# Seven products for eight in one projection of a decoder layer's finish, with two engines' order written by hand

## The chip, the cores and the metric

The kernel runs on one core of a Trainium2 chip. The metric is device microseconds of one execution, lower is better. Engines are named as the profile names them: PE is TensorE (PEld its weight loads), DVE is VectorE, ACT is ScalarE, POOL is GpSimd, SP is SyncE, which here issues nearly all DMAs. A line such as L258 is a line of the kernel before.

## What is computed

One decoder layer over 2048 tokens and 16 meta tokens, width 1024, in fp32. After an RMS norm and one wide input projection come two attention branches: stick-breaking attention (8 heads, width 512) and banded (sliding-window) attention with sinks (16 query heads, width 1024). The finish, cut to what matters here:

```python
y_sb = (o_sb * silu(sb_z)) @ w_branch_sb        # 512 -> 1024
y_sw = (o_sw * silu(sw_z)) @ w_branch_swa       # 1024 -> 1024, the banded branch
merged = sigmoid(g_sb) * y_sb + sigmoid(g_sw) * y_sw
h = h + merged @ w_out
return rms_norm(h, final_norm_gain)
```

## The kernel before

**Numbers.** Every fp32 operand of a matmul is split into a high and a low part of the type that TensorE takes at full rate: ScalarE copies (rounds) to `h`, VectorE subtracts to get `l`. A product of two operands is three matmuls: high by high, high by low, low by high. A matmul is 128 x 128 weights by 128 x 512 columns.

**Stages.** The tokens are four groups of 512 (`GT`), handled as two halves, `halves = ([2, 3], [0, 1])`. For both halves come the projections, the banded attention and the stick-breaking attention; their outputs (`ow` banded, `od` stick-breaking, two summands), the silu gates (`zw`, `zs`) and sigmoid gates (`gw`, `gs`) wait in HBM. Some gates of the first half are already computed by seven products for eight (`gate_pairs`, L1115). At the end of the second half's attention five gate weights are left (`gts[rest:]`, L1457), each for two groups: ten tiles of 24 matmuls (`gemm`, L457). In `use` (L613) ScalarE takes the sigmoid out of PSUM, VectorE multiplies for the last four weights (silu), and SP stores the tile. Beside them `gated` (L206) prepares the finish of half 0: it loads `ow` and `zw` into `tmp` buffers, which the gates use as well, multiplies them on VectorE and splits the result into two tiles of `ringl`, 32 tiles in all. `weights` (L178) splits a weight on ScalarE or GpSimd and also stores both parts in HBM (`kept`), so that half 1 loads them.

**The finish** (`finish`, L235) runs for half 0, then half 1. First the banded branch: for each of eight output tiles `d` of 128 features and each of the two groups, 8 k x 3 matmuls into one bank (`project`, L254; banks go round over three tags of two), then one VectorE multiplication with the gate `gw` gives `part[d, g]` (L286). `osb` holds the other branch's operands, made by `gated` at d = 3. Then `w_sb` for each d and group: project over 4 k, gate, add `part`, split into `merged` (L289 to L300), while `out_weights` (L265) loads and splits `w_out`. Then the output projection with residual and norm, in row tiles (L303 to L375). Half 1's operands are made by `gated_in_place` (L223) during half 0's output.

**What sets the order.** TensorE's order is the program's order throughout (`manual_schedule`). The order on the other engines, and on SP's queue, is laid down ahead of time by the planner, except in places where `manual_schedule` names an engine. Every queue is then worked in its order: an instruction that waits holds up those behind it. Buffers come from pools with a tag and a count (`bufs`): `ringl` 32 tiles, `ringr` 40, `small("a")` 6, `small("gt")` 3, `wh` and `wl` 3 each, `raw` 2, `tmp` 9, `xs` 4. The pool of `finish` lies where the normalised inputs `xh`, `xl` and `tmp` lay before.

## Time and profile before

| | |
|---|---|
| time, median of 3 runs | 2090.95 us (2090.8 to 2092.35) |
| profiled execution, its own time | 2093.26 us |
| its span | 2091.4 us |
| PE busy | 2076.3 us, 99% |
| DVE, ACT, POOL busy | 70%, 52%, 17% |
| granted TensorE clock | 0.999 |
| last five gates | 1593 to 1647 us |
| banded branch of half 0 | 1647.6 to 1734.6 us |

The span is the time from the first to the last instruction of the profiled execution. PE's busy time counts overlapping matmuls once. A busy share is an average over stages that have different limits, so what a stage can give is read in windows of time. "Idle before, releaser" in the rows names what ended an engine's wait.

### The profile page before, as it was taken

To read this page: it belongs to the slowest core of one execution; us is meant where nothing else is said; L and a number is where in the kernel's file an instruction comes from. 1 tells how busy PE (TensorE), PEld (TensorE's weight loads), DVE (VectorE), ACT (ScalarE), POOL (GpSimd) and SP (SyncE) were. 2 spreads that over 40 slices of the span, in tenths; PEclk is the share of its full clock that TensorE was granted. 3 is DMA by queue.
4 is the path that set the end of the run, shared out by engine and by line. 5 is a ranking of instruction groups with operands and counts; after the bars stand their busy time and mean duration, and the time that the engine had idled before them with its cause. 6 is when DMAs were issued, how large, how long until landed. Compare 5 with 4: busy or idle time off the path is not lost. (4 is left out here: it accounts for less than half of the span.)

```text
span 2091.4 us, 30949 instructions
## 1 busy us (share of the span) xinstructions
PE 2076.3 (99%) x10579; PEld 1744.8 (83%) x10579; DVE 1463.0 (70%) x2383; ACT 1091.4 (52%) x2657; POOL 345.7 (17%) x682
## 2 busy tenths in 40 slices
PE   9999999999999999999999999999999999999998
PEld 7888888888888888888888888888888888788887
DVE  7897986877687754887728788777774547464543
ACT  6677774577665335777735555655653212321121
POOL 1233444331000000233310000000000343000000
PEclk9999999999999999999999999999999999999999
DMA  9855555866377574435455344343424987568532
GB/s 338 307 195 201 188 175 179 252 199 185 91 278 298 209 247 163 159 126 177 150 171 161 120 130 129 114 129 98 121 83 165 350 318 223 182 229 305 154 100 91
DMA packets 170093, 391.46 MB, mean 187 GB/s; under 512 B 23728, under 2 KB 28208, under 8 KB 169936
## 3 DMA queue, kind: packets, MB, share of 16 engines
q1 hardware_dynamic: 169648, 389.23, 55.8%
q8 instruction: 83, 1.36, 0.3%
q14 instruction: 74, 0.61, 0.1%
q10 hardware_dynamic: 288, 0.27, 0.0%
HBM read 241.68 MB, written 145.18 MB: 185 GB/s over the span
## 5 line engine op out<-in xcount | busy, mean ns | idle before, releaser
L464 PE MATMUL ps_g<-xh,wh 128*128 128x512 f32 x1264 | 517.0, 409 | 1.1 <-DVE tmp L680 0.6
L464 PE MATMUL ps_g<-xl,wh 128*128 128x512 f32 x1264 | 495.6, 392 | 0.7 <-DVE xl L1199 0.6
L464 PE MATMUL ps_g<-xh,wl 128*128 128x512 f32 x1264 | 495.7, 392 | 0.0
L928 DVE TENSOR_TENSOR_SCAN row<-row 128x512 f32<-128x512 f32 (+4 forms) x256 | 290.1, 1134 | 116.2 <-POOL row L923 60.1
L464 PEld LDWEIGHTS ps_g<-xh,wl 128*128 128x128 f32 x1264 | 237.8, 188 | 52.7
L464 PEld LDWEIGHTS ps_g<-xh,wh 128*128 128x128 f32 x1264 | 238.5, 189 | 39.9 <-ACT xh L1198 1.4
L464 PEld LDWEIGHTS ps_g<-xl,wh 128*128 128x128 f32 x1264 | 239.2, 189 | 38.0 <-DVE xl L1199 1.8
L921 ACT ACTIVATE row<-ps_z 128x512 f32<-128x512 f32 (+4 forms) x352 | 175.1, 509 | 159.3 <-PE ps_z L918 155.0
L126 ACT ACTIVATE wth<-ps_t 128x512 fp32r<-128x512 f32 (+1 forms) x320 | 171.6, 536 | 61.4 <-PE ps_t L943 59.6
L127 DVE SCALAR_TENSOR_TENSOR wtl<-ps_t,wth 128x512 fp32r<-128x512 f32 (+1 forms) x320 | 188.7, 590 | 21.3 <-ACT wth L126 20.7
L918 PE MATMUL ps_z<-kt,q 128*128 128x512 f32 (+4 forms) x704 | 183.7, 349 | 2.0 <-ACT row L921 1.9
L943 PE MATMUL ps_t<-ident,row 128*128 128x128 f32 x1088 | 171.4, 273 | 1.0 <-DVE wtl L127 0.9
L943 PEld LDWEIGHTS ps_t<-ident,row 128*128 128x128 f32 x1088 | 134.5, 140 | 33.1 <-DVE wtl L127 1.8
L918 PEld LDWEIGHTS ps_z<-kt,q 128*128 128x128 f32 x704 | 124.4, 188 | 27.4 <-ACT row L921 5.1
L975 PE MATMUL ps_o<-wth,vc 128*128 128x512 f32 (+1 forms) x320 | 131.2, 410 | 0.0
L975 PE MATMUL ps_o<-wtl,vc 128*128 128x512 f32 (+1 forms) x320 | 116.4, 364 | 0.0
L767 ACT ACTIVATE sc<-sc,nm 128x129 f32<-128x129 f32 x256 | 100.0, 393 | 30.5 <-DVE nm L765 29.5
L934 POOL COPY mr<-row 128x16 f32<-128x16 f32 x128 | 28.4, 224 | 444.2 <-DVE row L928 401.8
L615 ACT ACTIVATE tmp<-ps_g 128x512 f32<-128x512 f32 x80 | 48.0, 600 | 80.5 <-PE ps_g L464 74.3
L299 ACT CAST ringl<-gt 128x512 fp32r<-128x512 f32 x32 | 19.9, 621 | 127.1 <-DVE gt L297 93.3
L117 POOL TENSOR_SCALAR wh<-raw 128x1024 fp32r<-128x1024 f32 (+1 forms) x45 | 49.8, 1108 | 212.7 <-PE ps_g L464 90.3
L123 POOL TENSOR_TENSOR wl<-raw,wh 128x256 fp32r<-128x256 f32 x88 | 83.2, 975 | 2.0
(442 smaller groups left out, 4202.3 us busy)
## 6 DMA issues: line engine op xcount, KB each, us to landing
wh<-h_in_w_in SPq DMA_DIRECT2D x66, 512.0 KB, 3.9
wl<-l_in_w_in SPq DMA_DIRECT2D x66, 512.0 KB, 5.1
h_in_w_in<-wh SPq DMA_DIRECT2D x50, 512.0 KB, 3.3
l_in_w_in<-wl SPq DMA_DIRECT2D x50, 512.0 KB, 4.1
raw<-in_w_in SPq DMA_DIRECT2D x49, 512.0 KB, 5.3
q<-qd SPq DMA_DIRECT2D x128, 128.0 KB, 3.2
vc<-vd SPq DMA_DIRECT2D x48, 256.0 KB, 3.2
kd<-tmp SPq DMA_DIRECT2D x32, 256.0 KB, 3.4
```

The lines of the kernel that those rows point to most:

```text
L117: G.tensor_scalar(h, src, 1.0, 1.0, op0=ALU.mult, op1=ALU.mult)
L123: G.tensor_tensor(l[:, c], src[:, c], f32(h[:, c]), op=ALU.subtract)
L126: A.activation(h, acc, AF.Copy, scale=scale)
L127: V.scalar_tensor_tensor(l, acc, scale, f32(h), op0=ALU.mult, op1=ALU.subtract)
L464: T.matmul(acc, lhsT=a[:, k, :], rhs=b[:, k, :], start=k == i == 0, stop=k == KT - 1 and i == 2)
L615: A.activation(e, acc, AF.Sigmoid)
L767: A.activation(sc[:, hh, :], sc[:, hh, :], AF.Exp, bias=nm[:, hh:hh + 1], accum_out=den[:, hh:hh + 1])
L918: T.matmul(z[:, :m], lhsT=qt[:, j * P:(j + 1) * P], rhs=kt[h][:, k0 + c:k0 + c + m], start=t == 0, stop=t == 1)
L921: A.activation(r[:, c:c + m], z[:, :m], AF.Sigmoid, scale=-1.0)
L928: V.tensor_tensor_scan(r[:, :w], r[:, :w], r[:, :w], last[j] if n else 1.0, op0=ALU.mult, op1=ALU.min)
L943: T.transpose(tr[:, j * P:(j + 1) * P], rows_of[h, g, n - (j > i), j][:, k0:k0 + P], ident)
L975: T.matmul(o[:, :n], lhsT=v, rhs=r, start=first and r is wh, stop=last)
```

## The change

For half 0 the banded branch is no longer computed as 16 independent tiles. Two output tiles d and d + 1 by the two groups ga and gb form a 2 x 2 square, and the 1024 features of k are cut in two halves of four (`HK`). Each square is a 2 x 2 by 2 x 2 block product, done with seven block products of 12 matmuls and sums of operands (Winograd's form): four squares, 28 products. `branch_by_pairs` holds TensorE's order, with sums left in a PSUM bank (`za`, `zb`, `x`) and continued by a later product.

- `outputs_blocks` makes the operands: for each of four k it loads four `ow`/`zw` pairs straight into ring tiles, multiplies, forms the sums t1 to t4 and splits them. Seven of these (t4 of every k, t3 of k = 2 and 3, t2 of k = 3) are written to HBM instead (`away`) and loaded and split later in `finish` (`late_split`).
- `weight_blocks` and `fill` make the weights' sums and split them on ScalarE and VectorE; GpSimd has no part in it. `w_sw` is no longer kept in HBM: half 1 loads it raw and splits it again (`keep=False`).
- A step of `outputs_blocks` (or a fill) follows each of the ten last gate tiles in program order. From the first of these to the branch's end ScalarE's and VectorE's order is the program's order.
- The other branch's operands (`other_branch`) are loaded and made between the products; the order of the gates' loads is written out (`gates`).
- `ringl` has 43 tiles, `ringr` 29; tiles of the branch's results and of `w_out` are shared out between them. `fg`'s load is moved behind the branch. In the `w_sb` loop tiles 0 and 1 go together, as (0, ga), (1, ga), (0, gb), (1, gb), and the last product of the branch stands behind the first of these. In half 1 loads of `w_sw` and `gw` are issued behind the last load of `w_out`.

```diff
-    def weights(c0, w=w_in, raw=None, split=split):
+    def weights(c0, w=w_in, raw=None, split=split, keep=True):
...
+        if not keep:
+            return wh, wl
...
+    def outputs_blocks(blk, away, k, ga, gb, ring, stg, free):
+        names = "b11", "b21", "t1", "b22"
+        here = [*names, "t2", "t3"][:(6, 6, 5, 4)[k]]
+        for name in here:
+            blk[name, k] = ring(), ring()
+        for name, kk, g in (("b11", k, ga), ("b21", k + HK, ga), ("t1", k, gb), ("b22", k + HK, gb)):
+            for t, src in zip(blk[name, k], (ow, zw)):
+                DMA(f32(t), src[kk][g])
+        yield
+        b11, b21, b12, b22 = (stg() for _ in names)
+        for t, name in zip((b11, b21, b12, b22), names):
+            a, z = blk[name, k]
+            V.tensor_tensor(t, f32(a), f32(z), op=ALU.mult)
+            if name in ("b11", "b21"):
+                part_split(*blk[name, k], t)
+        yield
+        t3 = free()
+        V.tensor_tensor(t3, b22, b12, op=ALU.subtract)
+        V.tensor_tensor(b12, b12, b11, op=ALU.subtract)
+        part_split(*blk["t1", k], b12)
+        part_split(*blk["b22", k], b22)
+        V.tensor_tensor(b22, b22, b12, op=ALU.subtract)
+        V.tensor_tensor(b21, b21, b22, op=ALU.subtract)
+        for name, t in (("t2", b22), ("t3", t3), ("t4", b21)):
+            if name in here:
+                part_split(*blk[name, k], t)
+            else:
+                away[name, k] = dram(f"{name}{k}", [P, GT])
+                DMA(away[name, k], t)
...
+        def gated_sum(d, g, acc):
+            t = part[d, g]
+            gt = gate_of(d, g)
+            V.tensor_tensor(t, acc, t, op=ALU.add)
+            V.tensor_tensor(t, t, gt, op=ALU.mult)
+        def close(d, z, w):
+            gt = gate_of(d, ga)
+            product(z, w, "t4", stop=True)
...
+            product(za, w[1], "t2")
+            keep(a, gb, za)
+            w = step()
+            product(x, w[0], "b22", stop=True)
+            gated_sum(a, gb, x)
+            middle()
+            product(za, w[1], "t3")
+            gated_sum(a + 1, gb, za)
+            w = step()
+            x = bank()
+            product(x, w[0], "t1", True)
+            keep(b + 1, gb, x)
+            middle()
+            close(a + 1, za, w[1])
...
+                def other_branch(k, g, ring):
+                    a, b, c = (small("a", AB) for _ in range(3))
+                    for t, src in ((a, od[k][g][0]), (c, od[k][g][1]), (b, zs[k][g])):
+                        DMA(t, src)
+                    V.tensor_tensor(a, a, c, op=ALU.add)
+                    V.tensor_tensor(a, a, b, op=ALU.mult)
...
-            osw = {}
-            todo = [(k, g) for g in halves[0] for k in range(8)]
...
+            byhand.enter_context(tc.manual_schedule(engines={mybir.EngineType.Activation, mybir.EngineType.DVE}))
+            next(side)
+            made_w = [gts[rest]()]
+            for mk in (*gts[rest + 1:], None):
+                if mk:
+                    made_w.append(mk())
+                w, use, _ = made_w.pop(0)
+                for g in groups:
+                    drain(lagged(col_tile(w, g, use)))
+                    next(side)
```

In the code `step` calls `before`, which makes the next fill of weights (fourteen fills, each for two products), and `middle` calls `during`, which holds the late splits and the other branch.

## The prediction

> **What bounds the kernel now.** I read the page's busy times first, then the windows around the stage that changes.

> ```profile
> span 2091.4 us, 30949 instructions
> ...
> PE 2076.3 (99%) x10579; PEld 1744.8 (83%) x10579; DVE 1463.0 (70%) x2383; ACT 1091.4 (52%) x2657; POOL 345.7 (17%) x682
> ```

> ```profile
> core 0: us, PE busy (x) PEld busy (x) DVE busy (x) ACT busy (x) POOL busy (x), PEclk, DMA share, GB/s
> 1590.00:1620.00 30.00, 30.00 (x136) 24.82 (x135) 7.85 (x12) 7.22 (x15) 0.00 (x0) 1.00 0.67 221
> 1620.00:1647.00 27.00, 27.00 (x121) 22.36 (x120) 18.59 (x24) 8.13 (x15) 9.97 (x10) 1.00 0.94 338
> 1647.00:1690.00 43.00, 43.00 (x192) 35.59 (x191) 20.64 (x25) 6.08 (x9) 19.50 (x20) 1.00 1.00 380
> 1690.00:1733.00 43.00, 43.00 (x191) 35.63 (x190) 15.94 (x20) 4.78 (x8) 13.88 (x16) 1.00 0.76 257
> 1733.00:1777.00 44.00, 44.00 (x195) 36.43 (x195) 38.19 (x52) 10.79 (x18) 15.87 (x18) 1.00 0.73 231
> 1777.00:1820.00 43.00, 42.44 (x184) 34.11 (x183) 18.42 (x39) 11.97 (x29) 0.00 (x0) 1.00 0.46 151
> 1862.00:1906.00 44.00, 44.00 (x196) 36.44 (x195) 27.24 (x53) 9.64 (x20) 0.00 (x0) 1.00 0.98 348
> ```

> TensorE (PE) is busy without a gap, at full granted clock, through the last five gates (to 1647), the banded branch (1647 to 1734) and the stage after it. So a matmul less is time less, as long as the others keep up. VectorE (DVE) is busy 26 of 57 us in the gates and 37 of 86 in the branch; the DMA engines are full in the first half of the branch (share 1.00, 380 GB/s). What a matmul costs is not its 389 ns, for matmuls overlap: it is the distance between starts.

> ```profile
> L258 PE MATMUL ps_g<-ringl,wh x96: 389/389/389, 1647.6 to 1953.1; 128*128 128x512 f32 x96
> ...
> L258 PE MATMUL ps_z<-ringr,wh x48: 389/389/389, 1734.6 to 1996.6; 128*128 128x512 f32 x48
> ```

> From the first banded matmul to the first of the other branch lie 87.0 us with 16 tiles x 24 = 384 matmuls: 0.2266 us each, 2.72 us for a product of twelve, 5.44 us for a tile of 24.

> **Term 1, the matmuls.** Four squares (two output tiles by two groups) of eight products become four of seven: 28 x 12 = 336 instead of 384. 48 x 0.2266 = **-10.9 us**. Bounds: nothing else can make this term larger; smaller only through waits, which follow.

> **Term 2, the last five gates.** Here VectorE's order is now the program's order, and it must multiply, combine and split all four k beside ten gate tiles of 5.44 us. Counted from the new code, VectorE has 14, 14, 13 and 12 operations for k = 0 to 3 (four products, two splits, four differences, two splits, and a split for each of t2, t3 that stays on the chip), 8 multiplications for the four silu gates, and 4 splits and 2 sums of weights: 67. ScalarE has 10 sigmoids, 21 copies of operands and 4 of weights: 35.

> ```profile
> 1610.37 0.69 DVE L217 TENSOR_TENSOR tmp<-tmp 128x512 f32<-128x512 f32 x1 [17.96 <-DMA tmp<-ow]
> ...
> 1621.20 0.69 DVE L217 TENSOR_TENSOR tmp<-tmp 128x512 f32<-128x512 f32 x1 [4.03 <-DMA tmp<-zw]
> 1622.58 0.69 DVE L220 TENSOR_TENSOR ringl<-tmp,ringl 128x512 fp32r<-128x512 f32 x1 [0.69 <-ACT ringl L219]
> ...
> 1632.34 0.69 DVE L220 TENSOR_TENSOR ringl<-tmp,ringl 128x512 fp32r<-128x512 f32 x1 [0.69 <-ACT ringl L219]
> 1632.95 0.69 DVE L217 TENSOR_TENSOR tmp<-tmp 128x512 f32<-128x512 f32 x1
> 1633.55 0.68 DVE L617 TENSOR_TENSOR tmp<-ps_g,tmp 128x512 f32<-128x512 f32 x1
> ```

> ```profile
> 1621.93 0.62 ACT L219 CAST ringl<-tmp 128x512 fp32r<-128x512 f32 x1 [5.59 <-DVE tmp L217]
> 1622.45 0.59 ACT L615 ACTIVATE tmp<-ps_g 128x512 f32<-128x512 f32 x1
> ```

> Back to back, VectorE starts an operation every 0.61 us (1632.34, 1632.95, 1633.55) and ScalarE every 0.52. A product that is split at once (1621.20, copy at 1621.93, difference at 1622.58) takes 1.38 from start to start, 0.77 more. Three splits of each k have nothing between them and their copy (b11, b21, t1). So VectorE needs 67 x 0.61 + 12 x 0.77 = 50.1 us. [...]

> When can it begin? That is a matter of SP's queue, which stays the planner's.

> ```profile
> 1594.58 1.10 SPq L59 DMA_DIRECT2D od<-tmp  x2
> ...
> 1604.05 0.33 SPq L59 DMA_DIRECT2D wh<-h_in_w_in  x1
> 1604.43 0.42 SPq L59 DMA_DIRECT2D tmp<-ow  x1
> ```

> ```profile
> tmp<-ow SPq DMA_DIRECT2D x16, 256.0 KB, 5.2
> ...
> h_in_w_sw<-wh SPq DMA_DIRECT2D x8, 512.0 KB, 5.4
> l_in_w_sw<-wl SPq DMA_DIRECT2D x8, 512.0 KB, 5.0
> gt<-gw SPq DMA_DIRECT2D x16, 256.0 KB, 5.6
> a<-od SPq DMA_DIRECT2D x16, 256.0 KB, 6.1
> ...
> zs<-tmp SPq DMA_DIRECT2D x8, 256.0 KB, 4.6
> a<-zs SPq DMA_DIRECT2D x8, 256.0 KB, 5.6
> ```

> Before, the first ow load stood behind a weight load that waited for a gate tile, and its tmp buffers are shared with the gates; VectorE sat idle until 1610. Now the loads go straight into 42 tiles of their own, which are free when the stick-breaking stage ends, and they are issued ahead of the first gate. I take them right behind the od store, 1595.7, landing 5 us later: start at 1600.7. 1600.7 + 50.1 = 1650.8. Of that the last five operations (a silu, two splits, two sums) aren't wanted until 5.4 us into the branch, -3.1; the stores of t2, t3 and t4 that go to HBM hold one of four xs buffers for some 5 us each and cost VectorE perhaps 1 us in each of three k, +3. So the first weights are ready near 1650.7, when the gates would end at 1647.6. Some of this slip is felt sooner: a silu multiplication now stands behind a whole step of the branch, and the gate's two PSUM banks wait for it. It is the same slip, not a second one. The ends: 0 if the loads land at once, 5 if the thirty-two of them (8.4 MB, 22 us at 380 GB/s) delay the stores. Value **+2.5 us**, near the worked 3.1.

> **Term 3, the branch.** 28 products, 76 us of TensorE. VectorE: 28 gate operations, 24 splits and 14 sums of weights, 7 late splits, 24 for the other branch: 97 x 0.61 = 59 us, and some 12 x 0.5 = 6 behind ScalarE's copies, 65 of 76. ScalarE: 51 copies, about 29 us. GpSimd's splits of w_sw are gone. Weights are two fills ahead (10.9 us), so they don't decide; the tightest place is the accumulator that lives on: t4's product may begin only when VectorE has read t3's sum out of the same bank, one product (2.72 us) later. That leaves VectorE about 1.9 us of lag (2.72 less 0.17 of pipeline and 0.69), at four places. VectorE lags whenever its next instruction waits for a transfer: the gates, 24 loads of od and zs into six buffers, two low halves. I take 0.5 us at each of the four, **+2.0 us**; ends 0 and 5 (VectorE's 11 us of slack half used up at the wrong moments). The DMA queue is eased: 16 writes of w_sw of 0.52 MB go, 14 transfers of 0.26 MB for t2 to t4 come, net 4.7 MB less.

> **Term 4, the rest of half 0.** In 1733 to 1777 VectorE is 38.19 of 44 us busy, and 0.56 us of TensorE are lost behind it in 1777 to 1820. Its work there is the same; it may start a little late. **+0.5 us**, ends -0.5 and +1.5. The first two w_sb weights are now wanted 5.4 us apart with t4's last product between; their slots come free 8.2 and 2.7 us before the first, and a split costs GpSimd 2.6 us (row below), so nothing.

> **Term 5, half 1.** w_sw is split anew instead of loaded.

> ```profile
> L123 POOL TENSOR_TENSOR wl<-raw,wh 128x256 fp32r<-128x256 f32 x48 | 43.5, 933 | 1.3
> L117 POOL TENSOR_SCALAR wh<-raw 128x1024 fp32r<-128x1024 f32 x8 | 9.8, 1221 | 83.2 <-PE ps_g L464 53.8 <-PE ps_g L259 21.7 <-DMA a<-zs 4.9
> L117 POOL TENSOR_SCALAR wh<-raw 128x512 fp32r<-128x512 f32 x8 | 6.0, 746 | 36.9 <-PE ps_z L259 14.0 <-PE ps_t L259 11.5 <-PE ps_g L259 11.4
> ```

> Four pieces of 0.93 us on an idle GpSimd and one wide copy on ScalarE (9.64 of 44 us busy) for each 10.9 us of TensorE: covered. DMA, at share 0.98 in 1862 to 1906, gets half the weight bytes. **0**, ends -0.3 and +1; if the cover went, a weight would be late once, by its 1.2 + 4 x 0.93 = 4.9 us. The moved load of fg and the other ring sizes (43 and 29 for 32 and 40) I cost at nothing: fg is first read in the output stage, behind the whole w_sb stage, and I counted 28 of 29 and 40 of 43 tiles alive at the worst points.

> **Sum.** -10.9 + 2.5 + 2.0 + 0.5 + 0 = -5.9 us. The profiled execution took 2093.26 us (span 2091.4), 2.3 more than the runs' median of 2090.95; 2087.4 against the former is **2085.0** for the median. The forecast's own ends: all waits nil and the old gap closed, 2079.5; all at their upper ends (5 + 5 + 1.5 + 1 = 12.5), 2092.5, which is unlikely together; I hold it to 2080 to 2090.

> **The rivals.**

> Late loads. If the planner again queues the first ow loads behind a gate's weights, VectorE starts at 1610 and not 1600.7, and there is no slack in the gates to make it up: 9 us more, less the 0.5 to 1 that then waits elsewhere, -5.9 + 8.5 = +2.6, **2093.5**. For it: that it happens in the trace. Against: the loads no longer need the gates' buffers. Chance 0.13.

> VectorE at 0.69 us an operation. 67 x 0.08 = 5.4 in the gates; 97 x 0.08 = 7.8 in the branch, 2 of them felt: -5.9 + 7.4 = +1.5, **2092.5**. [...] The 0.61 rows speak against it; chance 0.07.

> Slower: VectorE in order behind transfers. The place is the four xs buffers (three times, k = 1 to 3) and the six buffers of the od and zs loads (eight times). If a landing takes x us longer than the 5 I took, the gates lose 3x and the branch 8x less 11 of slack. With x = 2 that is 6 + 5 = 11: **2096**; with x = 2.5, 7.5 + 9 = 16.5: 2101.6. It outweighs the gain from 11x - 11 = 5.9, x = 1.5, landings of 6.5 us. For it: od took 6.1 us as a median in a full queue, and an instruction behind the waiting one can no longer pass. Against: the queue is lighter than before by 4.7 MB. [...] Chance 0.20, of which a part ends within 0.2%.

> **How the numbers follow.** Forecast 0.60, rivals 0.13, 0.07, 0.20. A measurement of this kernel can tell about 0.2% (4.2 us) from no change: 2086.8 and 2095.1. The forecast's range lies below 2086.8 for some 0.55 of its 0.60, and a little comes from rivals that cost less: faster 0.57. Same: 0.05 of the forecast, most of the first two rivals and some of the third, 0.22. Slower 0.21. The range from 2080 to 2097 holds the forecast, the first two rivals and the third up to x = 2.

> **What would show it.** Term 1: 336 matmuls of twelve-step products in some 76 us plus waits. Term 2: VectorE's first product near 1600, gate tiles still 5.44 us apart, the last gate's end at 1648 to 1651. Term 3: PE's waits name VectorE's sums at t4's products, under 1 us each. Term 4: VectorE near 38 of 44 us. Term 5: no PE wait on wh or wl in half 1. The prediction is wrong if gate tiles spread (late loads), or if VectorE's idle time in the branch is put down to od, zs or xs transfers in pieces of several us.

## The result, and the profile after

The changed kernel takes **2081.58 us** (median of five runs, 2080.57 to 2082.97) against 2090.96 (2090.8 to 2092.35) for the kernel before: 9.4 us less, ratio 0.9954 [0.9939, 0.9968]. The forecast was 2085.0, range 2080 to 2097. The profiled execution took 2080.66 us. Lines in this part are those of the changed kernel. First the head of its page, engines with busy time, share and instructions:

```profile
span 2078.7 us, 30974 instructions
...
PE 2064.4 (99%) x10531; PEld 1733.8 (83%) x10531; DVE 1507.8 (73%) x2467; ACT 1127.0 (54%) x2717; POOL 334.9 (16%) x674
```

There are 48 matmuls fewer (10579 before), and 84 instructions of VectorE and 60 of ScalarE more. The windows by stage, with the same columns as before:

```profile
core 0: us, PE busy (x) PEld busy (x) DVE busy (x) ACT busy (x) POOL busy (x), PEclk, DMA share, GB/s
1587.80:1646.00 58.20, 57.90 (x254) 46.70 (x251) 39.57 (x62) 20.38 (x38) 0.00 (x0) 1.00 0.75 271
1646.00:1720.80 74.80, 74.02 (x325) 60.58 (x324) 63.56 (x98) 31.29 (x54) 5.02 (x6) 1.00 0.77 257
1720.80:1767.20 46.40, 46.40 (x205) 38.20 (x204) 40.55 (x59) 14.00 (x23) 16.84 (x18) 1.00 0.77 243
1767.20:1854.30 87.10, 87.10 (x386) 72.09 (x386) 45.77 (x100) 26.85 (x65) 9.28 (x12) 1.00 0.62 213
1854.30:2078.70 224.40, 218.06 (x985) 181.37 (x983) 110.07 (x211) 50.48 (x109) 16.20 (x20) 1.00 0.48 154
```

The rows are the last five gates, 27 of the branch's 28 products, the last product with `w_sb`, the output of half 0, and half 1. In the branch VectorE is now busy 63.56 of 74.8 us, where it was busy 37 of 86.

The table gives these stretches for every kernel that was profiled, cut at the first matmul of each stage. "Gates" starts at the last transpose of the stick-breaking attention (L943 of before, L1249 of after); branch and `w_sb` stand together, since one product was moved across.

| kernel | gates | branch and w_sb | output, half 0 | half 1 | sum |
|---|---|---|---|---|---|
| before | 56.8 | 130.6 | 88.5 | 224.7 | 500.6 |
| after | 58.2 | 121.2 | 87.1 | 224.4 | 490.9 |
| eighth_product | 57.7 | 130.8 | 87.1 | 224.4 | 500.0 |
| planner_order | 56.8 | 123.3 | 87.0 | 224.4 | 491.5 |
| planner_gates_sums_later | 56.8 | 121.7 | 87.1 | 224.4 | 490.0 |
| gates_ten_more | 62.2 | 123.3 | 87.1 | 224.7 | 497.3 |
| branch_fifteen_more | 58.1 | 130.5 | 87.0 | 224.5 | 500.1 |
| sums_a_step_later | 58.0 | 121.1 | 87.1 | 224.4 | 490.6 |
| both | 61.0 | 121.9 | 87.1 | 224.4 | 494.4 |
| before_w_out_first | 56.9 | 130.5 | 87.1 | 224.5 | 499.0 |
| before_not_kept | 57.0 | 130.6 | 92.1 | 224.5 | 504.2 |
| not_kept_w_out_first | 56.9 | 130.5 | 87.1 | 224.5 | 499.0 |
| after_w_out_not_first | 58.2 | 122.0 | 96.4 | 224.4 | 501.0 |
| after_again | 58.2 | 121.2 | 87.1 | 224.4 | 490.9 |

The spans differ by 12.7 us, but 3.0 of that lie ahead of the first stretch (it begins at 1587.8 instead of 1590.8), in work that the change doesn't touch (over all these kernels this point lies between 1587.8 and 1590.8). From there on it is 500.6 - 490.9 = 9.7 us: +1.4 in the gates, -9.4 in branch and `w_sb`, -1.5 in the output of half 0, -0.3 in half 1. At 0.2266 us a matmul, branch and `w_sb` need 528 x 0.2266 = 119.6 us; 1.6 us are waits. The output's 384 matmuls need 87.0, so it has lost its waits altogether. Where PE's weight loads wait from the gates to the end, after (line waited for, us, times, longest):

```profile
engine line waited for: us in total, times, longest us
PEld ps_g L770 <- DVE tmp L923: 1.9, 4, 0.7
PEld ps_o L330 <- DVE ringl L341: 1.8, 3, 1.2
PEld ps_o L332 <- DVE wl L288: 0.2, 1, 0.2
```

The first row is the gates: a gate tile (L770) waits until VectorE's silu multiplication (L923) has read its bank. The second is t4's product, which waits for VectorE's sum with t3 (L341). The same view of before, within its output of half 0:

```profile
PEld ps_z L337 <- DVE ringr L270: 1.4, 3, 0.7
PEld ps_z L336 <- ACT ringr L269: 0.5, 1, 0.5
```

Lines 269 and 270 of before are the split of `w_out`. These waits are gone after.

### The profile page after: what moved, and what is told of

The parts are those of the page before. It is cut to its first block, busy times and chain, and to the rows that moved or that the text cites. A ratio compares the mean times of both kernels' runs of the same rounds, so it can differ in the third digit from the quotient of the medians.

```text
span 2078.7 us, 30974 instructions
## 1 busy us (share of the span) xinstructions
PE 2064.4 (99%) x10531; PEld 1733.8 (83%) x10531; DVE 1507.8 (73%) x2467; ACT 1127.0 (54%) x2717; POOL 334.9 (16%) x674
## 4 chain that ended last, share of the span: by engine, by line
PE 89%; DVE 4%; ACT 3%; DMA 2%; POOL 1%; issue 1%; SPq 0%; DVEq 0%; ACTq 0%; POOLq 0%
PE ps_g L770 36%; PE ps_o L1281 6%; PE ps_z L1224 6%; PE ps_t L1249 6%; PE ps_z L1065 3%; PE ps_o L1121 2%; PE ps_t L1099 1%; PE ps_z L770 1%; PE ps_g L644 1%; PE ps_g L642 1%; PE ps_g L643 1%; PE ps_z L440 1%; PE ps_t L440 1%; PE ps_z L438 1%; PE ps_t L438 1%; PE ps_t L439 1%
## 5 line engine op out<-in xcount | busy, mean ns | idle before, releaser
L770 PE MATMUL ps_g<-xh,wh 128*128 128x512 f32 x1264 | 516.4, 409 | 1.1 <-DVE tmp L986 0.6
L770 PE MATMUL ps_g<-xl,wh 128*128 128x512 f32 x1264 | 495.1, 392 | 0.7 <-DVE xl L1505 0.6
L770 PE MATMUL ps_g<-xh,wl 128*128 128x512 f32 x1264 | 494.8, 391 | 0.0
L770 PEld LDWEIGHTS ps_g<-xh,wl 128*128 128x128 f32 x1264 | 237.3, 188 | 52.6 <-DVE wl L119 0.2
L770 PEld LDWEIGHTS ps_g<-xh,wh 128*128 128x128 f32 x1264 | 238.1, 188 | 40.8 <-DVE tmp L923 1.9
L770 PEld LDWEIGHTS ps_g<-xl,wh 128*128 128x128 f32 x1264 | 238.7, 189 | 38.2 <-DVE xl L1505 2.0
L1249 PE MATMUL ps_t<-ident,row 128*128 128x128 f32 x1088 | 171.4, 273 | 1.0 <-DVE wtl L127 0.8
L1249 PEld LDWEIGHTS ps_t<-ident,row 128*128 128x128 f32 x1088 | 134.6, 140 | 33.1 <-DVE wtl L127 1.8
L123 POOL TENSOR_TENSOR wl<-raw,wh 128x256 fp32r<-128x256 f32 x88 | 80.8, 947 | 135.2 <-ACT wh L115 133.9
L654 ACT ACTIVATE sq<-res 128x512 bf16<-128x512 f32 (+1 forms) x33 | 20.4, 618 | 115.5 <-DVE res L646 113.4
L1232 DVE TENSOR_TENSOR_SCAN row<-row,mask 128x512 f32<-128x512 f32 (+2 forms) x64 | 70.0, 1100 | 17.4 <-ACT row L1227 16.9
## 6 DMA issues: line engine op xcount, KB each, us to landing
wh<-h_in_w_in SPq DMA_DIRECT2D x66, 512.0 KB, 4.0
wl<-l_in_w_in SPq DMA_DIRECT2D x66, 512.0 KB, 5.1
h_in_w_in<-wh SPq DMA_DIRECT2D x50, 512.0 KB, 3.3
l_in_w_in<-wl SPq DMA_DIRECT2D x50, 512.0 KB, 3.9
raw<-in_w_in SPq DMA_DIRECT2D x49, 512.0 KB, 5.2
vc<-vd SPq DMA_DIRECT2D x48, 256.0 KB, 3.0
kd<-tmp SPq DMA_DIRECT2D x32, 256.0 KB, 3.5
```

The costliest lines, as they stand in the source:

```text
L123: G.tensor_tensor(l[:, c], src[:, c], f32(h[:, c]), op=ALU.subtract)
L770: T.matmul(acc, lhsT=a[:, k, :], rhs=b[:, k, :], start=k == i == 0, stop=k == KT - 1 and i == 2)
L1232: V.tensor_tensor_scan(r[:, :w], r[:, :w], mask[:, :w], 1.0, op0=ALU.mult, op1=ALU.max)
L1249: T.transpose(tr[:, j * P:(j + 1) * P], rows_of[h, g, n - (j > i), j][:, k0:k0 + P], ident)
```

## The experiments

Each kernel was timed against the kernel before on the same chip; those medians were 2090.75, 2091.19 and 2090.9 in the three groups. Code and line numbers are those of the kernel that is changed.

### The 48 matmuls alone: eighth_product

```diff
             rest()
+            product(bank(), w[0], "b11", True, True)
...
             keep(b, ga, zb)
+            product(bank(), w[1], "b11", True, True)
```

> The kernel after with an eighth product put back into each of the four squares: the first product of each column is computed once more into a spare bank that nobody reads, 48 matmuls in all; the output stays the reference's. Theory (the gain is the 48 matmuls, 0.2266 us each): 10.9 us more than after, less up to 1.4 us of waits that TensorE's longer work now hides: 2091 to 2092.5 us, no faster than before. Rival (the gain comes from lighter transfers, moved loads or freed GpSimd, not from matmuls): it stays at 2082 to 2085 us.

Measured: 2090.74 us (2090.14 to 2091.9), ratio 1.000 [0.9991, 1.001]. With the 48 matmuls back, everything else of the change left as it is, the gain is gone. (The sum is 0.6 us below before: 1.4 less in the output and 0.3 in half 1, 0.9 more in the gates and 0.2 in the branch.) The matmuls are worth 500.0 - 490.9 = 9.1 us and not 10.9: with them branch and `w_sb` take 130.8 where 576 matmuls need 130.5, so the waits shrink from 1.6 to 0.3 us. The gates are 0.5 us shorter than after, though the edit doesn't touch them; why is open. The shorter branch waits 1.3 us more for VectorE than the same branch with the 48 matmuls.

### The order by hand: planner_order, planner_gates_sums_later

planner_order leaves VectorE's and ScalarE's order to the planner, save for ScalarE's in the last gate, as it was before:

```diff
-                hand.enter_context(tc.manual_schedule(engines={mybir.EngineType.Activation, mybir.EngineType.DVE}))
...
-            byhand.enter_context(tc.manual_schedule(engines={mybir.EngineType.Activation, mybir.EngineType.DVE}))
...
+                if mk is None:
+                    byhand.enter_context(tc.manual_schedule(engines={mybir.EngineType.Activation}))
```

> The kernel after with ScalarE's and VectorE's order given back to the planner, in the gates (but for ScalarE in the last one, as before) and in the branch. Theory: seven products carry the gain; the order by hand only keeps VectorE's lag off TensorE. The silu multiplications may pass the branch's work again, so the gates slip less (0 for 1.4 us), and the sums between t3 and t4 may be late instead (2 to 5 us for 1.4): 2081 to 2086 us. Rival (the order by hand is what makes the change pay): above 2088 us.

Measured: 2081.45 us (2080.8 to 2083.58), ratio 0.996 [0.9945, 0.9974], the time of the change itself. The gates then take 56.8 us, as before; branch and `w_sb` take 2.1 more. TensorE's waits from the gates to the end:

```profile
PE ps_o L330 <- DVE ringl L341: 1.6, 2, 1.0
PE ps_t L330 <- ACT ringl L336: 1.0, 1, 1.0
```

The order by hand costs 1.4 us in the gates and spares 2.1 in the branch; it isn't what pays. planner_gates_sums_later takes the better half of each: the planner in the gates, by hand in the branch, and the weight sums one step later (below).

> The kernel after with the planner's order for VectorE and ScalarE in the gates, the order by hand only in the branch, and the sums a step later. With the planner's order everywhere the gates took 56.8 us and the branch with the other branch 123.3. Theory (the two stretches add up): 56.8 and 120.0 to 120.8, the time 2 to 2.5 us below after. Rival (what the gates push back comes out at the branch's start, where the first weights or operands are late): 56.8 and 121.5 to 123, within 0.5 us of after.

Measured: 2081.71 us (2080.19 to 2082.62), ratio 0.9956 [0.9942, 0.9969]. The gain that the theory forecast did not come: the branch took 121.7 us where 120.0 to 120.8 were expected, as the rival had it. The stretches say 0.9 us less than after, the times nothing.

### How much room VectorE has: gates_ten_more, branch_fifteen_more

```diff
+            idle_t = tmp()
+            G.memset(idle_t, 0.0)
...
                     next(side)
+                    V.tensor_tensor(idle_t, idle_t, idle_t, op=ALU.add)
```

> The kernel after with one more VectorE addition of 128 x 512 (0.61 us from start to start) behind each of the ten steps in the gates, on a tile of zeros that nothing uses. Theory (from its first product VectorE has no slack in the gates: its order is a chain, and the silu multiplications at its end hold the gates' PSUM banks): nearly the whole 6.1 us comes out, the stretch from the last stick-breaking matmul to the branch grows from 58.2 to 62.5 to 64.5 us, the time to 2086 to 2088. Rival (VectorE is busy 39.6 of 58.2 us there, so it has room): at most 1 us more, 2081.5 to 2082.6.

Measured: 2088.57 us (2087.57 to 2089.57), ratio 0.9989 [0.998, 0.9998]. Ten additions beside the ten gate tiles are 10 x 0.61 = 6.1 us of VectorE; the gates take 4.0 us more and the branch 2.1. All of it is felt. The gates' stretch is 0.3 us below the theory's range and the time 0.6 above it; the theory had left out the branch. (`idle_t` is one of the gates' nine `tmp` tiles; no wait for such a tile shows.) TensorE's waits name the same lines as after, only longer:

```profile
PE ps_g L770 <- DVE tmp L923: 3.8, 5, 1.5
PE ps_o L330 <- DVE ringl L341: 2.1, 2, 1.6
```

branch_fifteen_more does the same at the end of each step of the branch, on `fg`, which isn't in use yet (and is filled first):

```diff
+        G.memset(fg[:, :GT], 0.0)
...
                     del after[:]
+                    V.tensor_tensor(fg[:, :GT], fg[:, :GT], fg[:, :GT], op=ALU.add)
```

> The kernel after with one more VectorE addition of 128 x 512 (0.61 us) at each of fifteen places in the branch, where a fill of weights has been made; 9.2 us in all. Theory (the branch leaves VectorE 11 us of slack, 63.6 busy of 74.8, and only the four places between t3's sum and t4's product are tight): a part comes out, 1 to 4 us, 2082.5 to 2085.6, as longer waits of t4's products. Rival (VectorE bounds the branch as it does the gates): 8 us or more, above 2089.

Measured: 2089.59 us (2087.26 to 2092.5), ratio 0.9992 [0.9983, 1.0001]. Fifteen additions are 9.2 us; branch and `w_sb` take 9.3 more. The theory of 11 us of slack fell. TensorE's timeline (start, duration, line, and in brackets the idle time before and what ended it):

```profile
1674.27 0.39 PE L332 MATMUL ps_g<-ringl,wl 128*128 128x512 f32 x1
1677.43 0.50 PE L330 MATMUL ps_o<-ringr,wh 128*128 128x512 f32 x1 [2.77 <-DVE ringl L341]
...
1679.00 0.63 PE L330 MATMUL ps_o<-ringr,wh 128*128 128x512 f32 x1
1679.42 0.63 PE L331 MATMUL ps_o<-ringr,wh 128*128 128x512 f32 x1
...
1682.34 0.39 PE L332 MATMUL ps_o<-ringl,wl 128*128 128x512 f32 x1
...
1719.93 0.50 PE L330 MATMUL ps_o<-ringr,wh 128*128 128x512 f32 x1 [1.75 <-DVE ringl L341]
...
1735.35 0.50 PE L330 MATMUL ps_o<-ringr,wh 128*128 128x512 f32 x1 [1.52 <-DVE ringl L341]
```

The longest waits stand at t4's product (L330 into `ps_o`), behind VectorE's sum; one of 1.16 us, at 1665.74, stands at a product that waits for a late split. And the longest costs more than itself: the fourteen distances from 1677.43 to 1682.34 take 4.91 us instead of 14 x 0.2266 = 3.17, because matmuls are 0.43 us apart for a while. The profiled execution is the slowest of this kernel's ten, so its 9.3 us is an upper end, and 1.7 of it are these slower matmuls; by the medians it is 8.0.

### Two waits taken away: sums_a_step_later, both

After, VectorE is held up once in the branch for longer. The place is one of the "two low halves" of Term 3: the sum L310 reads `res`, which is tile 3 of `w_sw`, loaded for the weights' sums. The timelines of SP and then of VectorE:

```profile
1652.09 0.43 SPq L59 DMA_DIRECT2D res<-in_w_sw  x1
```

```profile
1657.61 0.69 DVE L310 TENSOR_TENSOR a<-res 128x512 f32<-128x512 f32 x1 [3.41 <-DMA ringr<-t]
```

The row names a stored sum that is fetched back (`ringr<-t`), a load of the same queue; what the instruction reads is `res`, issued 5.5 us earlier, and in branch_fifteen_more the wait at the same line (4.6 us) is put down to `res<-in_w_sw`. sums_a_step_later makes this sum and the next one step later:

```diff
                         got["one"] = quarters(load(4 * P, w_sw))
-                        blocks.send((got["low2"], next_sum))
                     if n == 2:
+                        blocks.send((got["low2"], next_sum))
                         ahead.append(next(blocks))
```

> The kernel after with one edit: the two weight sums that read the low half of w_sw's tile 3 are made one step (two products) later. After has VectorE waiting 3.4 us for that tile at 1657.6, and the first t4 product 0.94 us late at 1671.5. Theory (VectorE's lag in the branch comes from waits for transfers in its order and isn't made up, as fifteen more operations showed): that stall goes, branch and other branch fall from 121.2 to 120.0 to 120.5 us, the time by 0.7 to 1.2. Rival (the lag comes from the number of operations): no change.

Measured: 2082.1 us (2081.52 to 2083.84), ratio 0.9959 [0.9946, 0.9971]. The wait of 3.41 us is gone, and t4's product now waits 0.6 in all. But the weight loads' waits have a new row:

```profile
PEld ps_t L330 <- ACT ringl L336: 1.2, 1, 1.2
PEld ps_o L330 <- DVE ringl L341: 0.6, 2, 0.3
```

A product now waits for ScalarE's copy out of the bank that it needs (`keep`, L336). Branch and `w_sb` take 121.1 instead of 121.2, where 120.0 to 120.5 were expected: one wait took the other's place.

both keeps this and also issues the gates' weights behind the first eight loads of `ow` and `zw`:

```diff
+                issued.append(DMA(f32(t), src[kk][g]).ins)
...
+                    with tc.issue_after(issued[7]):
+                        made_w.append(mk())
```

> The kernel after with the sums a step later, and the gates' weights queued behind the first eight ow and zw loads (before, 1 MB of weights wanted 20 us later goes ahead of them, and VectorE's first product waits until 1598.4). Theory (in the gates the slip is set by when VectorE can begin, as each of ten more operations came out): VectorE begins 2 to 2.6 us earlier, the gates take 57 to 57.3 us for 58.2, and with the branch's 0.7 to 1.2 the time falls 1.6 to 2.4 us below after. Rival (the start is set by HBM's queue whatever its order): 58.2 us in the gates and only the branch's part.

Measured: 2085.17 us (2084.28 to 2085.83), ratio 0.9972 [0.9961, 0.9984]: worse by 3.6 than the change, where 1.6 to 2.4 less were expected. VectorE does begin earlier, at 1597.01, 8.2 us into the gates instead of 10.6. But the weights that were put behind (issued from 1597.47) come late. Its TensorE timeline:

```profile
1604.49 0.47 PE L772 MATMUL ps_g<-xh,wh 128*128 128x512 f32 x1 [2.22 <-DMA wh<-h_in_w_in]
...
1605.66 0.51 PE L772 MATMUL ps_g<-xh,wl 128*128 128x512 f32 x1 [0.46 <-DMA wl<-l_in_w_in]
```

The gates take 61.0 us. The planner's order of this queue was the better one.

### The 1.5 us in the output of half 0: before_w_out_first, before_not_kept, not_kept_w_out_first, after_w_out_not_first

The changed kernel issues half 1's loads of `w_sw` and `gw` behind the last load of `w_out`. SP's timeline of before and then of after:

```profile
1778.13 0.32 SPq L59 DMA_DIRECT2D wh<-h_in_w_sw  x1
1778.54 0.38 SPq L59 DMA_DIRECT2D wl<-l_in_w_sw  x1
1780.36 2.35 SPq L59 DMA_DIRECT2D gt<-gw  x2
1782.77 7.23 SPq L59 DMA_DIRECT2D a<-in_w_out  x8
```

```profile
1765.44 10.54 SPq L59 DMA_DIRECT2D a<-in_w_out  x7
...
1778.89 0.42 SPq L59 DMA_DIRECT2D raw<-in_w_sw  x1
```

Before, `w_out`'s last eight loads are issued 4.6 us after the output's first matmul (1778.2), behind loads for half 1; after, seven of them from 1.8 us ahead of it (1767.2). before_w_out_first puts only this into the kernel before:

```diff
+                    with tc.issue_after(loaded[0]) if half else ExitStack():
+                        ws_of[d] = first if half == d == 0 else weights(d * P, w_sw)
...
+                with tc.issue_after(loaded[0]) if half else ExitStack():
+                    DMA(gt, gw[d][g])
```

> The kernel before with one part of the change: half 1's loads of w_sw and gw are issued behind the last load of w_out. The trace of before has 3 MB of w_sw and 0.8 MB of gw ahead of the eight w_out loads of the second column half, issued from 1782.8 us on and wanted from 1789. Theory (this queue costs the 1.5 us that half 0's output stage lost before and doesn't lose after): the output stage of half 0 falls from 88.6 to 87.1 us and the time to 2089 to 2090. Rival (the 1.5 us came with the other ring sizes or the paired tiles of w_sb): 88.6 us and 2091 as before.

Measured: 2089.42 us (2088.19 to 2090.5), ratio 0.9993 [0.9983, 1.0002]. The output takes 87.1 us, like after. The interval doesn't exclude no change; the stretch shows it.

before_not_kept takes only the other half, `w_sw` split anew, into the kernel before; not_kept_w_out_first takes both halves.

```diff
+        if not keep:
+            return wh, wl
...
+                    ws_of[d] = first if half == d == 0 else weights(d * P, w_sw, keep=False)
```

> The kernel before with one part of the change: w_sw is not written to HBM in half 0 (8.4 MB less) and is loaded raw and split again in half 1 (4.2 MB less). Theory (transfers were covered by TensorE): the branch stays 87.0 us, the time between 2089.7 and 2091.7, at best 1 us off the output stage because fewer bytes lie ahead of w_out. Rival (the lighter DMA queue is a source of the gain): 2087 us or less.

Measured: 2094.43 us (2091.94 to 2095.61), ratio 1.0017 [1.0008, 1.0027], slower; the output takes 92.1 us. Its SP timeline shows why:

```profile
1777.81 5.89 SPq L59 DMA_DIRECT2D gt<-gw  x3
1783.80 0.37 SPq L59 DMA_DIRECT2D raw<-in_w_sw  x1
1784.22 7.77 SPq L59 DMA_DIRECT2D a<-in_w_out  x8
```

A raw load waits for its buffer, which GpSimd's split still reads (SP's waits from 1755 to 1800 name L123 with 3.6 us in three), and `w_out` stands behind it. Neither the theory (2089.7 to 2091.7) nor the rival (2087 or less) had this. TensorE then waits for a split of `w_out` (its timeline), and the ten matmuls after this start 4.56 us apart in all instead of 2.27 (0.2 us of this is one more wait, before 1790.32):

```profile
1789.60 0.49 PE L338 MATMUL ps_z<-ringr,ringl 128*128 128x512 f32 x1 [2.60 <-ACT ringr L271]
...
1794.16 0.40 PE L339 MATMUL ps_z<-ringr,ringl 128*128 128x512 f32 x1
```

> The kernel before with two parts of the change together: w_sw not written to HBM but split again in half 1, and the loads of w_out ahead of those of w_sw and gw. Theory (splitting w_sw again costs TensorE nothing by itself; alone it lost 3.7 us only because its raw loads stood ahead of w_out): the output stage of half 0 is 87.1 us as with the second part alone, half 1 224.5, the time 2089 to 2090. Rival (the new splits cost time themselves, on ScalarE, VectorE or GpSimd): above 2091.

Measured: 2089.58 us (2088.23 to 2090.27), ratio 0.9992 [0.9983, 1.0002]; output 87.1, half 1 224.5. Splitting `w_sw` anew costs nothing, provided that its loads stay behind `w_out`'s.

after_w_out_not_first removes the two lines from the changed kernel:

```diff
-                    with tc.issue_after(loaded[0]):
-                        ws_of[d] = weights(d * P, w_sw, keep=False)
+                    ws_of[d] = weights(d * P, w_sw, keep=False)
...
-                with tc.issue_after(loaded[0]):
-                    DMA(gt, gw[d][g])
+                DMA(gt, gw[d][g])
```

> The kernel after without the order that holds half 1's loads of w_sw and gw behind the loads of w_out. Theory (without it they stand ahead of w_out in SP's queue, and wait there for buffers): half 0's output stage grows from 87.1 to 89 to 92 us, the time to 2083.5 to 2086.5. Rival (the order is only a precaution here): 87.1 us and 2081.6 as after.

Measured: 2089.29 us (2087.05 to 2092.14), ratio 0.9992 [0.9982, 1.0001]. The sign was expected, the size wasn't: 7.7 us more than the change, most of its gain. Its SP timeline, then TensorE's:

```profile
1773.79 4.73 SPq L59 DMA_DIRECT2D gt<-gw  x3
1779.50 0.33 SPq L59 DMA_DIRECT2D raw<-in_w_sw  x1
1779.88 6.81 SPq L59 DMA_DIRECT2D a<-in_w_out  x7
```

```profile
1772.99 0.39 PE L642 MATMUL ps_g<-ringr,ringl 128*128 128x512 f32 x1
1775.06 0.50 PE L640 MATMUL ps_g<-ringr,ringl 128*128 128x512 f32 x1 [1.68 <-ACT ringl L603]
...
1776.36 0.40 PE L641 MATMUL ps_z<-ringr,ringl 128*128 128x512 f32 x1
...
1781.38 0.39 PE L642 MATMUL ps_z<-ringr,ringl 128*128 128x512 f32 x1
1785.66 0.80 PE L640 MATMUL ps_t<-ringl 128*128 128x512 f32 x1 [3.89 <-ACT ringl L450]
...
1786.98 0.63 PE L642 MATMUL ps_t<-ringl 128*128 128x512 f32 x1
...
1791.25 0.56 PE L640 MATMUL ps_t<-ringr,ringl 128*128 128x512 f32 x1
1791.64 0.40 PE L641 MATMUL ps_t<-ringr,ringl 128*128 128x512 f32 x1
```

Counted from the output's first matmul, `w_out`'s loads are issued 13.2 us later than after (1779.88 is 11.4 behind 1768.5, and 1765.44 was 1.8 ahead of 1767.2). The 9.3 us that the output loses are three pieces: five distances from 1772.99 to 1776.36, 3.37 - 5 x 0.2266 = 2.2; the wait before 1785.66, 4.28 - 0.23 = 4.1; and then thirteen distances to 1791.64 that take 5.98 instead of 2.95, 3.0. The expectation had no third piece. The first is the same queue: VectorE's timeline, at the last gates of `w_sb`, shows a load of `gs` that comes late behind the raw loads.

```profile
1772.47 0.69 DVE L600 TENSOR_TENSOR gt<-ps_z,gt 128x512 f32<-128x512 f32 x1 [3.02 <-DMA gt<-gs]
```

The profiled execution took 2091.47 us, 2.2 above the median of its ten, so its pieces are an upper end here too.

### The changed kernel once more: after_again

> The kernel after, unchanged, beside the three that follow: 2081.6 us within 1, stretches of 58.2 us (gates), 121.2 (branch and the other branch), 87.1 (output of half 0), 224.4 (half 1) if their lengths are fixed by the order and not by chance. A rival that calls the gain of the first profile luck would see other lengths.

Measured: 2081.53 us (2081.21 to 2084.05), ratio 0.9958 [0.9946, 0.9971]. All stretches are those of the first profile to 0.1 us. So differences of stretches can be read to a few tenths, where times spread over 2 to 3 us. The single waits inside them do move: after, the first t4 product starts 0.94 us late (1671.50); here it starts 0.49 late (1671.97), and the fourth 0.45 (1724.46).

## Why the prediction was right, and where its steps were off

The direction and the mechanism held; the gain was 3.4 us larger than forecast. Over the stretches -5.9 was forecast and -9.7 measured; without the output's 1.5 us, which the forecast did not see coming, it would be -8.2.

**Term 1** holds: 48 matmuls of 0.2266 us are in the stretches, and eighth_product shows that without them nothing is gained. What "full rate" means for the split parts can be read in the trace of before: 512 columns of them take 0.2266 us from start to start, so 0.057 for 128, where the unsplit 128 x 128 transposes (L943) start 0.11 us apart.

**Term 2**, +2.5, measured +1.4. The operations were counted right: of VectorE's 67, 61 start before the branch does, where five were counted as not wanted yet, and of ScalarE's 35, 32. (The window's 62 and 38 also hold one and six operations that belong to the work before.) The number for the start was right too. VectorE's timeline after:

```profile
1598.39 0.69 DVE L261 TENSOR_TENSOR xs<-ringl 128x512 f32<-128x512 f32 x1 [9.01 <-DMA ringl<-zw]
1599.82 0.69 DVE L239 TENSOR_TENSOR ringl<-xs,ringl 128x512 fp32r<-128x512 f32 x1 [0.73 <-ACT ringl L238]
1600.43 0.69 DVE L261 TENSOR_TENSOR xs<-ringl 128x512 f32<-128x512 f32 x1
```

It begins 10.6 us into the gates; 1600.7 was 9.9 by the old clock. That it came so close was luck, since two errors cancel: the first load of `ow` was issued 3.0 us into the gates (1590.82), ahead of the store of `od`, where 4.9 was forecast, and VectorE began 7.1 us after the issue of the first `zw` (1591.24), where 5 was. The rival of late loads (1610, 19.2 us into the gates) didn't come, and neither did VectorE at 0.69 us: the last two rows start 0.61 apart. In the gates VectorE waits for none of the four `xs` buffers; the 3 us set down for them were too many. What slips is as described, a gate's bank behind a silu multiplication (1.9 us of weight loads' waits).

**Term 3**, +2.0, measured +1.6, at the place named: t4's product behind VectorE's sum. "Under 1 us each" held: counted by starts the longest is 0.94 us (the weight-load row's 1.2 is the wait of the load ahead of it). The operations of the branch, 97 of VectorE's and 51 of ScalarE's, are what the program has; the window's 98 and 54 hold a few of the gates' and lack a few of the branch's. What failed is the figure beside it, "VectorE's 11 us of slack". It was taken as total time less busy time. branch_fifteen_more shows that 9.2 us more of work cost 8.0 by the medians: little of VectorE's idle time can be used where TensorE needs it, at t4's products. The third rival's point of decision, 11x - 11, counted on this slack and so stood too high. The loads that it named cost next to nothing: none of the four `xs` buffers held VectorE up in the gates, and a load of `od` did so once in the branch, for 0.5 us. The longer wait (3.41 us) was for a tile of `w_sw`, and taking it away gained nothing.

**Term 4**, +0.5 with ends -0.5 and +1.5, measured -1.5, outside its ends. The step that failed is "0.56 us of TensorE are lost behind it": the size was read from PE's idle time in a window, where by the distances between starts the stage lost 88.5 - 87.0 = 1.5, and the loss was laid on VectorE without asking what VectorE waited for. The wait rows above name the split of `w_out`, and behind it stood SP's queue. The change lists that half 1's loads move behind `w_out`'s last; the prediction priced their splits, and gave the move itself no price. before_w_out_first shows this cause and its size; after_w_out_not_first shows that the changed kernel, whose raw loads wait for their buffer, would lose 7.7 us without the move. VectorE's share with `w_sb` was as forecast (40.55 of 46.4).

**Term 5**, 0, measured -0.3. No wait of PE names `wh` or `wl` in half 1, and not_kept_w_out_first shows the new splits to be free: 224.5 with them, as in before_w_out_first without them. gates_ten_more, which has the whole change, has the 224.7 of before too, so the 0.3 may be chance.

The differences, 1.1 in the gates, 0.4 in the branch, 2.0 in the output and 0.3 in half 1, are the 3.8 between -5.9 and -9.7. The best order tried, planner_gates_sums_later, still loses the 2.1 us of 121.7 over 119.6, and the times don't tell it from the change: no faster version was found, and whether some order of VectorE avoids that loss is open.

## What to carry to other kernels

Where TensorE is full, seven products for eight pay nearly what the matmuls cost (9.1 of 10.9 us here), but the shorter branch waits more for the engine that makes the sums (1.6 us here instead of 0.3): test its room by adding work, since span less busy time isn't room (9.2 us of additions cost 8.0, with 11 us counted as idle). When a stage's weights are no longer kept, look at where their loads stand in an in-order queue: the order that gains 1.5 us in the kernel before is worth 7.7 in the changed one. Price a loss in a window by the wait that ended it, not by the engine that was busiest there.

## What the runs showed of the hardware that was not expected

A stall of TensorE can cost nearly twice its length. After idle times of 2.60 us (before_not_kept), 2.77 (branch_fifteen_more) and 3.89 (after_w_out_not_first) matmuls were 0.43 us apart instead of 0.2266 for some 3 to 6 us (ten distances from 1786.98 to 1791.25 are 4.27), and 2.3, 1.7 and 3.0 us more were lost. The granted clock shows it. Here are two rows of branch_fifteen_more with the columns of the windows above; the wait of 2.77 us lies in the first:

```profile
1675.43:1678.84 3.41, 1.41 (x6) 1.19 (x7) 3.38 (x7) 0.00 (x0) 0.00 (x0) 1.00 0.61 197
1678.84:1682.25 3.41, 3.41 (x10) 2.62 (x9) 2.82 (x5) 0.98 (x2) 0.00 (x0) 0.50 0.78 220
```
